# A two-block sequence model on one core: modulation columns of the first block summed on TensorE, the delta rule's inverse loaded by another queue

## The chip, the cores and the metric

The kernel runs on one NeuronCore of a Trainium2 chip, as one launch. The metric is device time in microseconds (us); lower is better. The core's engines work at the same time, each through its own list of instructions in a fixed order, and wait for one another through semaphores. TensorE is PE in the profile (PEld is its weight load), VectorE is DVE, ScalarE is ACT, GpSimd is POOL, and SyncE is SP. SP here only starts transfers; POOL starts transfers too, on a queue of its own.

## The reference, cut to what matters

Two blocks follow one another. The change lies in the first, which works on 1024 latent tokens and 256 context tokens of width 1024:

```
silu_c = silu(c)
sh1, sc1, g1, sh2, sc2, g2 = split(silu_c @ w_mod + b_mod, 6)      # 6 vectors of 1024
h  = rmsnorm(x, norm1_g) * (1 + sc1) + sh1
zl = h @ w_in ;  zc = hc @ w_in                                     # one projection for all mixers
y  = concat([hyena(zl_hy), gla(zl_gla, zc_gla), gdn(zl_gdn, zc_gdn)]) @ w_out
x  = x + g1 * y
x  = x + g2 * square(relu(modulate(x, norm2_g, sh2, sc2) @ w_mlp1)) @ w_mlp2

# gdn: gated delta rule, 4 heads, forward and backward, in chunks
a   = -(k*beta) @ k.T * exp(strict lower decay)
sol = solve(eye - a, [k*beta*exp(gcum), v*beta])                    # triangular solve
w, u = sol                                                          # then a scan over chunks
```

Hyena is a long convolution done with discrete Fourier tables, GLA is a gated linear attention, gdn is the gated delta rule. All numbers are float32; matrix products that need it are split into a high and a low part.

## The kernel before, in words

**Modulation.** Of the six vectors, four (g1, sc2, sh2, g2) are made by `mods1` with `mod_block`, one column block of 1024 of `w_mod` each. A column block comes in eight row blocks `mr` (128 x 1024, 512 KB), and with the `"pool"` setting ACT scales a block by its entry of silu(c) (L268), POOL adds it to a running sum `ma` (L391; the first of eight is written by ACT as `ma` itself), and at the end PE sums `ma` over partitions with eight products of a 128x128 piece of `ma` as weight and a column of ones (the trace's `px<-consts,ma`; each float32 product is two instructions). `mr` lies in two slots of the tag `wr`, `ma` in a slot of `wh`; both tags hold the weights of the projection before that and of the output product after.

**The delta rule.** `gdn_pre` first builds the strict matrices and stores them in HBM (`gdnU`, `gdnE`). Then, in the stage called E below, it goes over four heads h and two directions d, eight chains in all. Per head it loads keys and values (`st`, 96 x 1280, from SP), transposes them on PE into rows `rk` and `rv` (one buffer each). Per direction POOL makes `nk = rk * nbg` and `W = rv * beta` (L1240, L1241), and `gdn_E` loads `U` (L1144, from SP) and builds the inverse E by doubling the block size, 16 to 32 to 64 to 128: short products on PE (`D,U`, `E,Z`, `Ec,Z`), each followed by a copy on ACT or DVE, which the next products need. Then products with W and nk follow (`W,E`, `E,nk`), whose results POOL stores (`gdn_W` L1249, `gdn_GT` L1256). The end of `gdn_GT` is the end of a chain.

**What lies around it.** Hyena's Fourier products (`fh,TF`, `fl,TF`, `gh,TI`, `gl,TI`, with splits on DVE at L287) have their own input and no part in the delta rule; so have the modulation and, later, GLA's products (`eq`, `ek`, `v`, `at`, `kr`). The scan of the delta rule (two passes, W added at L1327, rows at L1351) needs all of E. Its result `orowsd` gets a head norm (ACT squares `hnj`, POOL L966), is transposed on PE, goes to HBM (`yT`, L979) and back as the input of the output product WO (`pm<-wo,cl` and `ch`).

**What sets the order.** The code is run at build time through a scheduler that puts each engine's instructions in one list, by priority and by when buffers come free. Every list is then executed in order. So an edit in one place shifts work of other parts in all lists: which Hyena, modulation or GLA products stand between two links of an E chain is decided there.

Of the kernel before, what the change touches and what calls it, by code (L numbers as in the profile page):

```python
# [19 lines left out]
D = 1024  # L20
# [3 lines left out]
KT = 8  # L24
# [142 lines left out]
class Builder:  # L167
# [204 lines left out]
    def mod_block(self, tl, w, b, cvs, outs, eng="dve"):  # L372


        nc, nv = self.nc, len(cvs)
        acc = [tl(f"ma{v}", 1, (128, D)) for v in range(nv)]
        for k in range(KT):
            raw = tl("mr", 2, (128, D))
            nc.sync.dma_start(out=raw, in_=w[k * 128 : (k + 1) * 128, :])
            for v in range(nv):  # L380
                cv = cvs[v][:, k : k + 1]
                if v == 0 and eng == "dve":
                    if k == 0:
                        self.ts(acc[0], raw, cv, ALU.mult)
                    else:
                        self.stt(acc[0], raw, cv, acc[0], ALU.mult, ALU.add)
                elif k == 0:
                    self.act(acc[v], raw, AF.Copy, scale=cv)
                else:
                    self.act(raw, raw, AF.Copy, scale=cv)  # L390
                    nc.gpsimd.tensor_add(out=acc[v], in0=acc[v], in1=raw)  # L391
            yield
        p = self.ps()
        for v in range(nv):
            for j in range(8):
                self.mm(p[:, v * 8 + j : v * 8 + j + 1], acc[v][:, j * 128 : (j + 1) * 128], self.ones[:, 0:1])
        for v in range(nv):
            nc.vector.tensor_add(out=outs[v], in0=p[:, v * 8 : v * 8 + 8], in1=b)
        yield
# [740 lines left out]
    def gdn_E(self, h, d, tl, ps, Ud, Ed, E, D1, Ec):  # L1140

        nc, V = self.nc, self.nc.vector
        U = tl("U", 2, (128, 10, 128))
        nc.sync.dma_start(out=U, in_=Ud[h, d].rearrange("c j i -> j c i"))  # L1144
        blk = lambda b: slice(b * 32, b * 32 + 32)
        v32 = lambda p: p[:, :320].rearrange("p (c t) -> p c t", t=32)
        flat = lambda t: t.rearrange("p c t -> p (c t)")
# [52 lines left out]

    def gdn_rows(self, src, dst):

        for c0 in range(0, 10, 5):
            p = self.ps()
            for i in range(5):
                self.tp(p[:, i * 96 : i * 96 + 96], src[:, (c0 + i) * 128 : (c0 + i + 1) * 128])
            self.act(dst[:, c0 : c0 + 5], p[:, :480].rearrange("p (c d) -> p c d", d=96), AF.Copy)

    def gdn_pre(self, dr, gt):
# [12 lines left out]
        with ExitStack() as es:  # L1222
# [6 lines left out]
            for h in range(4):  # L1229
                rows = []  # L1230
                for n in "kv":
                    t, r = tl("st", 2, (96, TT)), tl("r" + n, 1, (128, 10, 96))
                    nc.sync.dma_start(out=t, in_=dr[n][h * 96 : h * 96 + 96])
                    self.gdn_rows(t, r)
                    rows.append(r)
                for d in range(2):
                    E = Es[d]
                    f = lambda n: gt[n][:, d * 40 + h * 10 : d * 40 + h * 10 + 10].unsqueeze(2).broadcast_to([128, 10, 96])
                    nk, W = tl("nk", 1, (128, 10, 96)), tl("W", 2, (128, 10, 96))
                    nc.gpsimd.tensor_mul(out=nk, in0=rows[0], in1=f("nbg"))  # L1240
                    nc.gpsimd.tensor_mul(out=W, in0=rows[1], in1=f("beta"))  # L1241
                    self.gdn_E(h, d, tl, self.ps, Ud, Ed, E, D1[d], Ec[d])
                    G = tl("G", 1, (96, 10, 128))
                    for c0 in range(0, 10, 5):
                        p = self.ps()
                        for i in range(5):
                            self.mm(p[:, i * 96 : i * 96 + 96], E[:, c0 + i], W[:, c0 + i])
                        self.act(W[:, c0 : c0 + 5], p[:, :480].rearrange("p (c d) -> p c d", d=96), AF.Copy)
                    nc.gpsimd.dma_start(out=dr["W"][h, d], in_=W)  # L1249
                    for c0 in range(0, 10, 4):  # L1250
                        n = min(4, 10 - c0)
                        p = self.ps()
                        for i in range(n):
                            self.mm(p[:96, i * 128 : i * 128 + 128], nk[:, c0 + i], E[:, c0 + i])
                        self.act(G[:, c0 : c0 + n], p[:96, : n * 128].rearrange("p (c t) -> p c t", t=128), AF.Copy)
                    nc.gpsimd.dma_start(out=dr["GT"][h, d], in_=G)  # L1256
# [310 lines left out]
    def mods1(self, tl):  # L1567
# [2 lines left out]
        m = {}  # L1570
        for j, nm in ((2, "g1"), (4, "sc2"), (3, "sh2"), (5, "g2")):
            t = self.const(nm, [128, 8])
            for _ in self.mod_block(tl, A["w_mod"][0][:, j * D : j * D + D], self.c["b_mod"][:, j * 8 : j * 8 + 8], [c], [t], "pool"):
                pass
            m[nm] = self.col_row(nm + "row", t) if nm[0] == "g" else t
        m["gs2"] = self.gs_cols("gs2", m["sc2"], self.c["norm2_g"])
# [134 lines left out]
    def block1(self, x3, ey):  # L1711
# [16 lines left out]
        with ExitStack() as e1:  # L1728
# [60 lines left out]
            with ExitStack() as es:  # L1789
# [3 lines left out]
                ep.enter_context(self.psums(px=4))  # L1793
                with ExitStack() as eh:
                    hl = self.tiler(self.pool(eh, "hym"))
                    ml = lambda tag, bufs, shape: self.wp.tile(list(shape), F32, name=self.nm(tag), tag={"mr": "wr", "ma0": "wh"}[tag], bufs=2)
                    eh.enter_context(self.smalls())
                    self.hy_mix(F, dr["hy"], yT, hl)
                    pmix, self.pools = self.pools, pmod
# [692 lines left out]
```

## Time and profile before

| what | value |
|---|---|
| median of 3 runs | 3723.88 us (3720.07 to 3733.52) |
| profiled execution | 3723.89 us |
| span in its trace | 3722.1 us |
| mean granted TensorE clock | 0.914 |
| PE busy | 3350.3 us, 90% of the span |
| DVE, ACT, POOL busy | 63%, 42%, 36% |

The profiled execution is at the median, and its span is shorter than its time by 1.8 us. In the views a granted clock of 1 is 2.4 GHz and 0.5 is 1.2 GHz; a value between them is a mean over a stretch with both. The chain that ended last is given by the page for the whole span and only reaches back to about 1005 us; the stages of the first block before that are read from windows. In this execution the last product of the first block's projections ends at 626 us.

### The profile page before, as it was taken

How to read it: one execution, taken by the hardware profiler on the slowest of the kernel's cores; microseconds unless marked ns; L12 is line 12 of the kernel's file. 1: busy time of each engine (PE TensorE's matmuls, PEld its weight loads, DVE VectorE, ACT ScalarE, POOL GpSimd, SP SyncE). 2: the span in 40 equal slices, each digit the busy share in tenths (PEclk: the TensorE clock that was granted, in tenths of full speed). 3: DMA queues.
4: the chain of work that ended last, by engine and by line, in shares of the span. 5: the costliest groups of instructions: out<-in, count | busy, mean ns of one | idle time of the engine just before them, and what ended most of it. 6: DMA issues, size and time to landing. Idle time of an engine off the chain costs nothing.

```text
span 3722.1 us, 53759 instructions
## 1 busy us (share of the span) xinstructions
PE 3350.3 (90%) x19966; PEld 2797.4 (75%) x19966; DVE 2339.3 (63%) x4512; ACT 1563.9 (42%) x3045; POOL 1350.8 (36%) x1182
## 2 busy tenths in 40 slices
PE   6899998667796999999999799998899999998897
PEld 5567877567785777777788678887788778876785
DVE  8696452667457466456544756665677756664776
ACT  4454345533324252222211434444466554444663
POOL 3233344553546433234422201112555511113554
PEclk9799998767655999999999899999999999998998
DMA  7544544744313553222221111113444421124443
GB/s 258 183 143 148 141 127 148 236 153 140 106 42 102 187 183 92 70 88 91 85 84 47 62 38 57 50 50 90 138 121 144 156 63 60 49 66 137 116 134 139
DMA packets 350098, 421.24 MB, mean 113 GB/s; under 512 B 58388, under 2 KB 273860, under 8 KB 349837
## 3 DMA queue, kind: packets, MB, share of 16 engines
q1 hardware_dynamic: 323372, 322.21, 29.2%
q0 software_dynamic: 26464, 95.58, 7.0%
q8 instruction: 159, 2.61, 0.3%
q14 instruction: 103, 0.84, 0.1%
HBM read 317.96 MB, written 99.76 MB: 112 GB/s over the span
## 4 chain that ended last, share of the span: by engine, by line
PE 47%; DVE 10%; issue 5%; DMA 4%; ACT 4%; POOL 3%; SPq 0%; POOLq 0%; ACTq 0%; DVEq 0%
PE pm L256 28%; PE px L256 13%; PE pa L256 2%; PE po L256 1%; PE px L265 1%; PE pa L265 1%; DMA mr<-in_w_ada 1%; DVE ma L271 1%; ACT e L268 1%; DVE amx L2376 1%; DVE e L287 1%; DVE x L287 1%; DMA wr<-qd 1%; POOL ma L391 0%; POOL cl L287 0%
## 5 line engine op out<-in xcount | busy, mean ns | idle before, releaser
L256 PE MATMUL pm<-x,wh 128*128 128x512 f32 (+3 forms) x4768 | 1427.6, 380 | 2.3 <-DVE x L287 2.3
L256 PEld LDWEIGHTS pm<-x,wh 128*128 128x128 f32 (+2 forms) x4768 | 865.4, 189 | 164.3 <-issue 5.9
L256 PE MATMUL pm<-x,wl 128*128 128x512 f32 (+3 forms) x2384 | 909.4, 382 | 30.0 <-ACT u L268 21.0
L256 PEld LDWEIGHTS pm<-x,wl 128*128 128x128 f32 (+2 forms) x2384 | 451.7, 190 | 117.6 <-ACT u L268 21.7
L256 PE MATMUL pm<-wo,ch 128*128 128x512 f32 x832 | 267.3, 402 | 0.0
L287 DVE TENSOR_TENSOR wl<-wr,wh 128x1024 fp32r<-128x1024 f32 (+1 forms) x110 | 143.3, 1303 | 164.1 <-ACT wh L268 163.8
L1654 DVE TENSOR_TENSOR oa<-px,oa 128x512 f32<-128x512 f32 x240 | 161.7, 688 | 130.0 <-PE px L256 129.9
L391 POOL TENSOR_TENSOR ma<-ma,mr 128x1024 f32<-128x1024 f32 x63 | 160.5, 2548 | 178.5 <-ACT mr L268 154.0
L256 PE MATMUL px<-w2h,ml 128*128 128x512 f32 x480 | 195.4, 407 | 25.0 <-DVE ml L287 25.0
L268 ACT ACTIVATE u<-pm 128x512 f32<-128x512 f32 (+2 forms) x204 | 108.5, 543 | 258.0 <-PE pm L256 229.7
L256 PE MATMUL px<-w2h,mh 128*128 128x512 f32 x480 | 192.6, 401 | 0.0
L256 PE MATMUL px<-w2l,mh 128*128 128x512 f32 x480 | 192.1, 400 | 0.0
L256 PEld LDWEIGHTS pm<-wo,ch 128*128 128x128 f32 x832 | 160.1, 193 | 32.1 <-issue 0.2
L275 POOL TENSOR_SCALAR mkw<-kr,gws 128x128 f32<-128x128 f32 x144 | 80.7, 565 | 284.0 <-PE px L256 235.4
L256 PE MATMUL pm<-wo,cl 128*128 128x512 f32 x416 | 169.7, 408 | 9.9 <-POOL cl L287 8.0
L2376 DVE TENSOR_REDUCE amx<-pa 128x1 f32<-128x640 f32 (+2 forms) x144 | 107.4, 746 | 73.6 <-PE pa L256 72.5
L268 ACT ACTIVATE wh<-wr 128x1024 fp32r<-128x1024 f32 (+2 forms) x138 | 143.3, 1038 | 18.4 <-PE pm L256 13.9
L268 ACT ACTIVATE e<-e 128x1280 f32<-128x1280 f32 (+3 forms) x126 | 134.1, 1068 | 39.9 <-DVE e L275 36.8
L268 ACT ACTIVATE w2h<-wr 128x1024 fp32r<-128x1024 f32 x32 | 33.9, 1058 | 269.1 <-PE px L256 232.7
L268 ACT ACTIVATE P<-pa,amx 128x640 f32<-128x640 f32 (+2 forms) x144 | 105.6, 734 | 95.2 <-DVE amx L275 84.9
L268 ACT ACTIVATE mr<-mr,silu_cc 128x1024 f32<-128x1024 f32 x63 | 72.3, 1148 | 149.7 <-DVE ma L271 113.6
L1552 POOL TENSOR_TENSOR xr<-or,xr 128x512 f32<-128x512 f32 x72 | 93.4, 1297 | 103.0 <-DVE or L1551 87.0
(899 smaller groups left out, 7392.6 us busy)
## 6 DMA issues: line engine op xcount, KB each, us to landing
wr<-in_w_in SPq DMA_DIRECT2D x102, 512.0 KB
wr<-in_w_mlp SPq DMA_DIRECT2D x64, 512.0 KB
mr<-in_w_ada SPq DMA_DIRECT2D x48, 512.0 KB
TF<-dft SPq DMA_DIRECT2D x54, 384.0 KB
mr<-in_w_mod SPq DMA_DIRECT2D x32, 512.0 KB
xp<-xr POOLq DMA_DIRECT2D x26, 512.0 KB, 4.0
xr<-xp SPq DMA_DIRECT2D x26, 512.0 KB
wr<-in_w_out SPq DMA_DIRECT2D x24, 512.0 KB
```

Source lines behind the costliest of these rows:

```text
L256: self.nc.tensor.matmul(out, a, b, start=start, stop=stop)
L265: self.nc.tensor.transpose(out, in_, self.ident[:p, :p])
L268: self.nc.scalar.activation(out, in_, f, **kw)
L271: self.nc.vector.scalar_tensor_tensor(out=out, in0=in0, scalar=scalar, in1=in1, op0=op0, op1=op1)
L275: (eng or self.nc.vector).tensor_scalar(out=out, in0=in0, scalar1=s1, scalar2=s2, op0=op0, **kw)
L287: (leng or self.nc.vector).tensor_sub(out=lo, in0=src, in1=hi.bitcast(F32))
L391: nc.gpsimd.tensor_add(out=acc[v], in0=acc[v], in1=raw)
L1552: nc.gpsimd.tensor_add(out=xr[:, fs], in0=r, in1=xr[:, fs])
L1654: V.tensor_add(out=oa[t][:, fs], in0=p, in1=oa[t][:, fs])
L2376: V.reduce_max(m_, s[:, w0:768], axis=AX.X)
```

## The change

There are four edits. With `"pe"`, `mod_block` sums on TensorE: each 128x128 piece of a row block `mr` is the weight of a product with the one matching column of silu(c), eight pieces for each of eight row blocks, 64 columns of PSUM in all, which DVE reduces over k and adds the bias to. ACT's scaling and POOL's sums are gone for these four vectors. The row blocks take turns in the two tags `wr` and `wh` of two slots each. `U` is loaded by POOL's queue. `rk` and `rv` have two buffers each and are loaded in halves, and for d = 1 POOL scales them in place, where before a separate `nk` and `W` were written.

```diff
 def mod_block(self, tl, w, b, cvs, outs, eng="dve"):
+        if eng == "pe":
+            p = self.ps()[:, :64]
+            for k in range(KT):
+                raw = tl(k, (128, D))
+                nc.sync.dma_start(out=raw, in_=w[k * 128 : (k + 1) * 128, :])
+                for j in range(8):
+                    self.mm(p[:, j * 8 + k : j * 8 + k + 1], raw[:, j * 128 : (j + 1) * 128], cvs[0][:, k : k + 1])
+                yield
+            nc.vector.reduce_sum(outs[0], p.rearrange("p (j k) -> p j k", k=KT), axis=AX.X)
+            nc.vector.tensor_add(out=outs[0], in0=outs[0], in1=b)
+            yield
+            return
...
 def gdn_E(self, h, d, tl, ps, Ud, Ed, E, D1, Ec):
-        nc.sync.dma_start(out=U, in_=Ud[h, d].rearrange("c j i -> j c i"))
+        nc.gpsimd.dma_start(out=U, in_=Ud[h, d].rearrange("c j i -> j c i"))
...
 def gdn_rows(self, src, dst):
-        for c0 in range(0, 10, 5):
+        for c0 in range(0, dst.shape[1], 5):
...
 def gdn_pre(self, dr, gt):
-                    t, r = tl("st", 2, (96, TT)), tl("r" + n, 1, (128, 10, 96))
-                    nc.sync.dma_start(out=t, in_=dr[n][h * 96 : h * 96 + 96])
-                    self.gdn_rows(t, r)
+                    r = tl("r" + n, 2, (128, 10, 96))
+                    for c0 in (0, 5):
+                        t = tl("st", 2, (96, 640))
+                        nc.sync.dma_start(out=t, in_=dr[n][h * 96 : h * 96 + 96, c0 * 128 : c0 * 128 + 640])
+                        self.gdn_rows(t, r[:, c0 : c0 + 5])
...
-                    nk, W = tl("nk", 1, (128, 10, 96)), tl("W", 2, (128, 10, 96))
+                    nk, W = rows if d else (tl(t, 1, (128, 10, 96)) for t in ("nk", "W"))
...
         for j, nm in ((2, "g1"), (4, "sc2"), (3, "sh2"), (5, "g2")):
             t = self.const(nm, [128, 8])
-            for _ in self.mod_block(tl, A["w_mod"][0][:, j * D : j * D + D], self.c["b_mod"][:, j * 8 : j * 8 + 8], [c], [t], "pool"):
+            for _ in self.mod_block(tl, A["w_mod"][0][:, j * D : j * D + D], self.c["b_mod"][:, j * 8 : j * 8 + 8], [c], [t], "pe"):
...
                     hl = self.tiler(self.pool(eh, "hym"))
-                    ml = lambda tag, bufs, shape: self.wp.tile(list(shape), F32, name=self.nm(tag), tag={"mr": "wr", "ma0": "wh"}[tag], bufs=2)
+                    ml = lambda k, shape: self.wp.tile(list(shape), F32, name=self.nm("mr"), tag=("wr", "wh")[k % 2], bufs=2)
```

What this does to the lists shows at three places. The first is PE at the end of the chain of head 1, direction 1. Before, the links of the chain (`px_46..`, products with E, Z, nk and W) stand between Hyena's products (TF, TI):

```order
L256 MATMUL px_4643<-E_781_3684,Z_4561 64x64 x5
L256 MATMUL px_4651<-W_4454,E_781_3684 128x96 x5
L256 MATMUL px_8288<-fh_8284,TF_8282 128x512
L256 MATMUL px_8310<-gh_8304,TI_8308 128x256
...
L256 MATMUL px_8288<-fl_8285,TF_8282 128x256
L256 MATMUL px_8288<-fh_8284,TF_8282 128x256
L256 MATMUL px_4658<-W_4454,E_781_3684 128x96 x5
L256 MATMUL px_4666<-E_781_3684,nk_4453 96x128 x4
```

In the changed kernel the same links have products of the modulation (`silu_cc,mr`) between them as well as Hyena's:

```order
L256 MATMUL px_9248<-silu_cc,mr_9279 128x1 x2
L256 MATMUL px_4647<-E_781_3684,Z_4565 64x64 x5
L256 MATMUL px_4655<-rv_4210,E_781_3684 128x96 x5
L256 MATMUL px_9248<-silu_cc,mr_9279 128x1
L256 MATMUL px_8450<-gh_8444,TI_8448 128x512
L256 MATMUL px_9248<-silu_cc,mr_9279 128x1 x2
L256 MATMUL px_9248<-silu_cc,mr_9289 128x1 x7
L256 MATMUL px_8450<-gl_8445,TI_8448 128x512
L256 MATMUL px_8450<-gh_8444,TI_8448 128x512
L256 MATMUL px_8450<-gh_8444,TI_8448 128x256
L256 MATMUL px_8450<-gl_8445,TI_8448 128x256
L256 MATMUL px_4662<-rv_4210,E_781_3684 128x96 x5
```

Hyena is further on at this place (its product 8450 against 8288), and all products of the modulation, 256 against 32, stand between the last projection and the end of the last chain; the rest of Hyena's, which before stood in the scan (107 of 300 rows), stand there too.

The second is POOL around the same chain. Before, the running sums `ma` stand between the multiplications of the delta rule and its stores:

```order
L391 TENSOR_TENSOR ma_1748_9150<-ma_1748_9150,mr_9178 128x1024
L1249 DMA gdn_W<-W_4224 128x960
L391 TENSOR_TENSOR ma_1760_9199<-ma_1760_9199,mr_9203 128x1024
L1240 TENSOR_TENSOR nk_4453<-rk_4190,gnbg_2320 128x960
L1256 DMA gdn_GT<-G_4420 96x1280
```

In the changed kernel no sum is left, and the loads of U (L1156) stand between:

```order
L1156 DMA U_4729<-gdnU 128x10x128
L1263 DMA gdn_W<-W_4230 128x960
L1270 DMA gdn_GT<-G_4426 96x1280
L420 DMA g1row<-crow_9243 8x128
L1156 DMA U_4957<-gdnU 128x10x128
L1263 DMA gdn_W<-rv_4210 128x960
L1270 DMA gdn_GT<-G_4654 96x1280
L1254 TENSOR_TENSOR nk_4725<-rk_4687,gnbg_2320 128x960
L1254 TENSOR_TENSOR rk_4687<-rk_4687,gnbg_2320 128x960
L1255 TENSOR_TENSOR W_4726<-rv_4706,gnbeta_2277 128x960
L1255 TENSOR_TENSOR rv_4706<-rv_4706,gnbeta_2277 128x960
```

A load of U for a later chain stands ahead of the stores of the chain that runs, and the four multiplications of a head (in place for d = 1) follow one another.

The third is PE between the end of the scan and WO. Before, the last transposes of `orowsd` are followed by GLA's products, 195 with eq and ek and 33 with v, S or kr among them, and the first product of WO comes after the last of them:

```order
L265 MATMUL px_8174<-consts,orowsd 128x128 x4
L256 MATMUL px_10561<-eq_10473,k_10026 128x128 x4
L256 MATMUL px_10596<-v_10035,at_1962_10334 128x96
...
L256 MATMUL pq_10658<-eq_10648,ek_10649 32x32
L256 MATMUL pq_10659<-eq_10648,ek_10649 32x32
L256 MATMUL pm_10276<-wo_1930_10212,cl_10269 128x512
```

In the changed kernel the scan's last products (S, W, qs) and the transposes stand directly ahead of WO:

```order
L256 MATMUL px_8051<-S_8029,qs_7692 128x96
L256 MATMUL px_8051<-W_8041,at_7691 128x96
L265 MATMUL px_8143<-consts,orowsd 128x128
...
L265 MATMUL px_8173<-consts,orowsd 128x128
L265 MATMUL px_8182<-consts,orowsd 128x128
L256 MATMUL pm_10448<-wo_1926_10384,cl_10441 128x512
```

GLA's products that stood here are in the scan now (496 rows with eq and ek there against 293), except the last twelve steps of the scan, which have none between them.

## Rows read from the trace of the kernel before

**Rows 1.** The page: busy us per engine, share of the span, instructions.

```profile
PE 3350.3 (90%) x19966; PEld 2797.4 (75%) x19966; DVE 2339.3 (63%) x4512; ACT 1563.9 (42%) x3045; POOL 1350.8 (36%) x1182
```

**Rows 2.** Windows: busy us (instructions) per engine, then clock, DMA share, GB/s.

```profile
627.00:858.00 231.00, 161.15 (x2185) 146.48 (x2186) 149.47 (x212) 103.72 (x182) 124.46 (x65) 0.67 0.60 188
858.00:988.00 130.00, 93.12 (x592) 85.01 (x590) 92.11 (x179) 40.01 (x79) 55.29 (x29) 0.77 0.50 141
988.00:1132.00 144.00, 137.15 (x1111) 119.11 (x1109) 73.90 (x192) 41.91 (x83) 67.24 (x48) 0.60 0.17 45
1132.00:1202.00 70.00, 42.42 (x457) 34.45 (x456) 53.56 (x70) 32.83 (x114) 51.14 (x33) 0.56 0.30 96
```

**Rows 3.** Line L1256, the store that ends each chain: ns, first and last start.

```profile
L1256 POOL DMA_DIRECT2D gdn_GT<-G x8: 523/547/710, 564.3 to 858.2; - x8
```

**Rows 4.** Waits, 627 to 858: us in total, times, longest.

```profile
PEld px L256 <- issue: 44.4, 15, 11.0
...
PE px L256 <- DVE D L1162: 22.6, 3, 10.9
```

**Rows 5.** Tile ma, window 627 to 858: columns as in rows 2.

```profile
627.00:858.00 231.00, 9.41 (x64) 9.55 (x64) 0.00 (x0) 3.43 (x3) 62.29 (x25) 0.67 0.60 188
```

**Rows 6.** Timelines of PE from 750 and from 803: start, duration.

```profile
750.60 1.84 PE L256 MATMUL px<-consts,ma 128*128 128x1 f32 x16
...
803.07 3.57 PE L256 MATMUL px<-consts,ma 128*128 128x1 f32 x16
```

**Rows 7.** Windows of 20 and 40 us: columns as in rows 2.

```profile
1060.00:1080.00 20.00, 20.00 (x223) 17.84 (x222) 10.58 (x28) 6.07 (x13) 8.25 (x7) 0.50 0.17 41
720.00:740.00 20.00, 16.14 (x186) 14.03 (x186) 15.95 (x27) 13.84 (x24) 9.48 (x4) 0.83 0.74 233
1220.00:1260.00 40.00, 40.00 (x221) 32.52 (x218) 16.84 (x26) 6.26 (x10) 17.02 (x17) 1.00 0.60 207
```

**Rows 8.** Tiles TF, then TI, window 858 to 988: PE, PEld, clock, DMA.

```profile
858.00:988.00 130.00, 11.50 (x45) 9.13 (x45) 0.77 0.50 141
...
858.00:988.00 130.00, 13.22 (x59) 10.59 (x57) 0.77 0.50 141
```

**Rows 9.** One DVE group by form, 627 to 858, then 858 to 988: busy, mean ns.

```profile
L287 DVE TENSOR_TENSOR gl<-t,gh 128x512 fp32r<-128x512 f32 x13 | 15.7, 1211 | 5.5 <-ACT gh L268 5.4
...
L287 DVE TENSOR_TENSOR gl<-t,gh 128x512 fp32r<-128x512 f32 x5 | 3.4, 682 | 0.8 <-ACT gh L268 0.8
```

**Rows 10.** Lines L1144 (U's load, SP) and L1109 (U's store, POOL): issue, ns min/median/max.

```profile
L1144 SPq DMA_DIRECT2D U<-gdnU x8: 370/376/5219, 481.3 to 777.6; - x8
...
L1109 POOL DMA_DIRECT2D gdnU<-U x8: 954/982/1418, 391.2 to 450.7; - x8
```

**Rows 11.** Groups by form, 1132 to 1202, PE, then ACT: busy, mean ns, idle before.

```profile
L265 PE MATMUL px<-consts,orowsd 128*128 128x128 f32 x24 | 6.2, 429 | 0.0
...
L256 PE MATMUL px<-v,kr 128*64 128x96 f32 x40 | 4.1, 365 | 11.8 <-ACT kr L268 7.8 <-DVE hnr L307 4.0
...
L268 ACT ACTIVATE hnj<-orowsd 128x96 f32<-128x96 f32 x29 | 7.8, 269 | 0.0
L268 ACT ACTIVATION_READ_ACCUMULATOR hnj<-orowsd 128x1 f32 x29 | 5.5, 189 | 0.0
```

**Rows 12.** Timeline of POOL, 1130 to 1203: start, duration, idle before.

```profile
1160.50 7.67 POOL L966 TENSOR_TENSOR orowsd<-orowsd,hnr 128x384 f32<-128x384 f32 x8 [0.82 <-DVE hnr L307]
...
1195.95 1.56 POOL L898 TENSOR_TENSOR eq<-eq,q 128x512 f32<-128x512 f32 x1 [10.39 <-ACT eq L268]
...
1200.88 1.54 POOL L287 TENSOR_TENSOR cl<-wr,ch 128x640 fp32r<-128x640 f32 x1
```

**Rows 13.** The chain that ended last, around 1290: start, duration, what.

```profile
1288.01 6.38 DMA yT<-hng
1294.53 2.90 DMA wr<-yT
```

**Rows 14.** Line L1327 in the scan, 934 to 953: ns, first and last start.

```profile
L1327 DVE TENSOR_TENSOR W<-px,W x8: 347/358/358, 936.2 to 951.0; 128x192 f32<-128x192 f32 x8
```

## The prediction

> **What bounds the kernel now.** I read the page first. PE is busy nine tenths of the span and no other engine comes near it [rows 1], so the whole kernel is a list of PE's work with a few holes, and an edit can only be worth what it adds to that list or what it takes from the holes. The page's slices put the holes between a sixth and a third of the span, so next I cut that part into windows by stage [rows 2]: from the end of the projections to the end of the last E chain (627 to 858), the scan's part with Hyena beside it (858 to 988), the scan's part with GLA beside it (988 to 1132), and from the scan's end to the first product of WO (1132 to 1202). PE is idle there for 69.9, 36.9, 6.9 and 27.6 us, 141 of 575. All four edits act inside these 575 us. What comes after them has the same work as before, but for 8 GLA products fewer, so I take its time as unchanged.
>
> In the E stage the eight chains end between 564 and 858 us [rows 3], six of them behind the projections, so one takes 31 to 48 us. PE waits there for short copies that the next link of the chain needs: 22.6 us for D on DVE in three waits, and 44.4 us of weight loads wait for something that the profile does not show [rows 4]. PE does not wait for the modulation. So the chain of links, with whatever stands between them in PE's list, sets this stage.
>
> **The change part by part.** All sums are made in the time of the profiled execution, 3723.89 us, which is the median of the runs within 0.01 us.
>
> *Modulation on PE.* The order has 256 products where there were 32, all of them in the E stage. A product is two instructions, so 448 instructions are new. Before, 64 of this shape (a 128x128 weight, one column) took 9.41 us of that window, 0.147 us each [rows 5]. That mean lies between two levels in the timeline: 16 of them took 1.84 us at one place, 0.115 each, and 3.57 us at another, 0.223 each [rows 6], the ratio of the two clock levels. So the new work costs 448 x 0.147 = 65.9 us, with bounds of 51.5 and 99.9 us. I take the mean of the stage, because the new products are spread over all of it as the old ones were. What goes in exchange is POOL's sums and ACT's scaling, 62.3 us of POOL in this window [rows 5]; PE had no wait for these, so I count them at nothing directly.
>
> *What POOL's silence gives.* While POOL adds, some DVE operations of the same shape are longer: Hyena's low part `gl` took 1211 ns in the E stage and 682 ns in the scan [rows 9]. That is 13 x 0.53 = 7 us on DVE for this group. It shortens waits and not PE's work; I put it into the idle time below.
>
> *Hyena moves forward.* In the order none of Hyena's products is left in the scan. In the trace those were 11.50 + 13.22 = 24.7 us of PE [rows 8]. The E stage gets them and the scan loses them.
>
> *The E stage, summed.* PE's work becomes 161.2 + 65.9 + 24.7 = 251.8 us, more than the 231 us that the stage has. The idle time of 69.9 us cannot stay, because at most links there are now products to do. Some must stay, because the list is in order: a product that stands behind a link cannot go ahead of it, and six chains have about ten links each. I take 25 us, about 4 us for each chain; bounds are 0 and the old 69.9. The stage is then 276.8 us, **+45.8 us**.
>
> *U's load by POOL's queue, rows in two buffers and in place.* SP's issue of U's load took 0.37 us, once 5.2 us; POOL's issue of the store of the same tensor took about 1 us [rows 10]. Eight of these are 8 us on an engine that loses 62 us of sums, so the cost is nothing while POOL has slack. In POOL's list they stand ahead of the stores of the chain that is running, which then wait too if U's buffer is not free. The doubled rows let a head's transposes and multiplications be done while the head before it is still in its chains; this takes a start-up wait from each head, and I count that in the 25 us too. With the cover gone, a load of U that is late holds the first link of a chain: that is a rival below.
>
> *The scan.* Of 274 us PE was busy for 93.1 + 137.2 = 230.3. It loses Hyena's 24.7. It gains the GLA products that stood between the scan's end and WO: the 42.4 us of that window [rows 2] less the 6.2 us of the transposes, which stay [rows 11], 36.2 us. That makes 241.8 us. Of the idle 43.8 us I keep 33: GLA's products now fill more steps, but the last twelve steps have nothing beside them. Such bare steps were in the trace too; eight additions of W between 936.2 and 951.0 [rows 14] give about 2.1 us for a step, most of it PE's own. The scan is then 274.8 us, **+0.8 us**, with bounds of -17 (15 us idle) and +19. The upper one is the clock: if the part from 858 on falls from 0.77 to the 0.60 of the next window when Hyena leaves, its other 68.4 us of work grow by 28%, 19 us.
>
> *The scan's end to WO.* What held WO for 70 us was GLA's work in all lists: PE's products, and POOL's `eq` ahead of the split `cl` that WO's first product reads [rows 12]. PE alone waited 11.8 us for GLA's `kr` [rows 11]. With that work gone ahead, the head norm's own chain is left: the squares on ACT, 7.8 + 5.5 = 13.3 us if none is done in the scan [rows 11], POOL's scaling 7.67 us [rows 12], four transposes at 0.43 us, the store to `yT` with its landing 6.38 and the load back 2.90 [rows 13], the split 1.54 us: 33.5 us. Without the squares it is 20 us, but the small steps of the norm's root, not in this sum, come on top. I take 33 us, **-37 us**, with bounds of -50 and -20.
>
> The sum is 45.8 + 0.8 - 37 = +9.6 us: **3734 us**.
>
> **The rivals.**
>
> *The clock rises (faster).* The E stage ran at a granted clock of 0.67 on average. Where Hyena's wide products were dense it was 0.83, with PE busy for 16.1 of 20 us [rows 7]. If filling the holes brings the whole stage to that, its other work of 161.2 + 24.7 = 185.9 us shrinks by 0.67/0.83 to 150 us, the modulation costs its lower bound of 51.5, and with 25 us idle the stage is 226.5 us, 4.5 us less than before. With the scan and the tail as above that is -41 us: 3683 us. Against it: PE was busy for all of 1060 to 1080 at a clock of 0.50, with GLA's narrow products, and for all of 1220 to 1260 at 1.00 with WO's wide ones [rows 7]. So being busy did not by itself raise the clock here, and the new products are the narrowest of all. It decides from a stage mean of about 0.75 on. The Trainium skill, "TensorE: Matmul & The Clock Gate", section "What's actually happening", says that the default state is throttled and that activity releases it, to 2.4 GHz; by that rule this rival would be the forecast. The trace does not agree at 1060 to 1080, where PE has no hole and stays at the lower level.
>
> *The holes take everything.* The chance to be near 0 idle in the E stage: 251.8 us, +20.8, with the other terms -15.4 us: 3708 us. For it speaks that the new products wait for nothing but a load made long before; against it, the order of the list.
>
> *Half clock throughout (slower).* If the new products come in groups between links where the clock is low, as at 803 us, they cost 99.9 instead of 65.9 us: +34, 3768 us. It decides when more than half of them take over 0.2 us.
>
> *U late on POOL (slower).* If each load of U after the projections waits as long as SP's longest, 5.2 us, with the stores and the next head's multiplications behind it, six chains lose 31 us: 3765 us. Against it: POOL's queue has 62 us less to do, and the loads stand a chain ahead.
>
> *The tail keeps another holder.* If WO comes only 20 us earlier, for its low bound above, the total is 3751 us.
>
> **How the numbers follow.** About 0.5% (18.6 us) is what a measurement of this kernel can tell from no change; so faster is under 3705 and slower over 3742. The forecast, from 3715 to 3753 by the idle time in the E stage and in the scan, has a chance of 0.40; 0.30 of it lies within the bound and 0.10 above. The clock's rise has 0.24, all faster. The holes that take everything have 0.10, 0.06 of it faster. Half clock has 0.16, U late and the tail 0.05 each, all slower. That is 0.30 faster, 0.34 the same, 0.36 slower. For the range I go to the clock's rise below and to half clock above, each with some room for the scan's bounds: 3675 to 3785. The likeliest case's own range is 3715 to 3753.
>
> **What the profile would show.** *Modulation:* 512 instructions of one column with silu(c) in the E stage, their mean between 0.12 and 0.22 us, and PE's busy time there over 240 us; if the mean is at 0.115 and the stage's clock above 0.75, the clock's rise was right. *E stage:* its end (the last `gdn_GT`) about 46 us later, near 904, and PE idle in it under 30 us. *POOL:* no `ma`; if its waits ahead of the load of U are longer than a few us, and PE waits for that load, U is late. *DVE:* `gl` near 0.7 us in the E stage. *Scan:* from the last `gdn_GT` to its last W about 275 us. *Tail:* 33 us from there to WO's first product, with no GLA product in it, and the head norm and the transfer of `yT` as what is waited for. The forecast is wrong if the E stage's end moves by less than 20 us or more than 70, or if the tail stays over 50 us.

## The result and the profile after

The changed kernel takes 3787.27 us (median of 4 runs, 3775.92 to 3793.42) against 3728.70 us of the kernel before on the same chip: a ratio of 1.0149, 95% interval 1.0125 to 1.0173. It is slower by 1.5%, 58.6 us. The profiled execution after took 3781.57 us with a span of 3779.8, 57.7 us more than the span before, so the two traces show nearly all of the difference.

I cut both traces at the same events: the end of the projections, the last `gdn_GT` store, the last row that DVE adds to `orowsd`, the first product of WO, the end.

| stage | before, us | after, us | difference | forecast |
|---|---|---|---|---|
| up to the end of the projections | 625.8 | 627.6 | +1.8 | 0 |
| E stage | 232.4 | 288.7 | +56.3 | +45.8 |
| scan | 274.0 | 295.5 | +21.5 | +0.8 |
| scan's end to WO | 70.3 | 43.0 | -27.3 | -37 |
| from WO on | 2519.6 | 2525.0 | +5.4 | 0 |

From WO on I had forecast no change. In the traces of the experiments below this part (the span less the start of WO's first product) lasts between 2521 and 2530 us whatever the edit, so these 5.4 us can't be told from no change.

The page's first line after the change. PE's busy time grew by 89 us, POOL's fell by 71:

```profile
PE 3439.7 (91%) x20414; PEld 2885.2 (76%) x20414; DVE 2304.4 (61%) x4516; ACT 1533.2 (41%) x3013; POOL 1279.4 (34%) x1162
```

Windows by stage, with the columns of [rows 2]:

```profile
627.00:916.00 289.00, 264.17 (x2833) 249.01 (x2831) 166.23 (x290) 89.59 (x182) 74.51 (x48) 0.66 0.54 176
916.00:1212.00 296.00, 249.70 (x2040) 219.04 (x2040) 161.59 (x365) 91.61 (x201) 140.47 (x96) 0.66 0.24 64
1212.00:1255.00 43.00, 6.53 (x25) 4.47 (x26) 17.06 (x20) 16.03 (x68) 25.08 (x19) 0.53 0.50 161
```

In the E stage PE is idle for 24.8 us, where it was idle for 69.9 [rows 2]: the holes were filled, and the work that filled them was larger than the holes. The first row below gives that work; the second, the store that ends each chain, answers to [rows 3] with its last start 58 us later:

```profile
L256 PE MATMUL px<-silu_cc,mr 128*128 128x1 f32 x512 | 87.8, 299 | 0.0
...
L1270 POOL DMA_DIRECT2D gdn_GT<-G x8: 521/531/533, 564.3 to 916.3; - x8
```

512 instructions in 87.8 us are 0.171 each (the 299 ns are the overlapping durations of single ones). The weights' loads take as long, 89.3 us of PEld beside 87.8 of PE. The granted clock of the stage hardly moved, 0.66 for 0.67. The new products are found at both levels again, as in [rows 6]; in the timeline of PE after, 0.213 us each in the first row and 0.116 in the second:

```profile
821.60 2.98 PE L256 MATMUL px<-silu_cc,mr 128*128 128x1 f32 x14
...
844.31 1.62 PE L256 MATMUL px<-silu_cc,mr 128*128 128x1 f32 x14
```

Windows of 30 us show where the scan gained idle time: in its first 60 us, after the change and before it, with the columns of [rows 2].

```profile
916.00:946.00 30.00, 12.57 (x70) 11.74 (x70) 8.23 (x20) 7.00 (x12) 14.30 (x10) 0.60 0.81 221
946.00:976.00 30.00, 15.31 (x195) 13.08 (x197) 24.05 (x42) 9.18 (x17) 22.80 (x13) 0.65 0.22 64
```

```profile
858.00:888.00 30.00, 24.53 (x138) 21.64 (x136) 24.12 (x42) 12.74 (x26) 9.27 (x5) 0.77 0.70 205
888.00:918.00 30.00, 21.91 (x141) 19.86 (x142) 27.49 (x46) 10.26 (x20) 13.34 (x7) 0.89 0.30 77
```

PE is idle for 32.1 us there, before for 13.6. The timeline after says what it waits for. SP's list has GLA's tables and first loads ahead of the scan's keys; all are issued only after the last store of the E stage, and PE stands until the keys have landed:

```profile
918.90 0.33 SPq L210 DMA_DIRECT2D consts<-in_consts  x1
919.28 0.77 SPq L827 DMA_DIRECT2D v<-gla_v  x1
920.15 1.10 SPq L831 DMA_DIRECT2D lk<-gla_log  x1
921.30 0.43 SPq L1293 DMA_DIRECT2D k<-gdn_k  x1
...
932.12 1.83 PE L265 MATMUL px<-consts,k 96*128 96x96 f32 x10 [17.14 <-DMA k<-gdn_k]
```

SP's own waits from 890 to 945 after the change say what held it: GLA's tables (`consts`), ahead of the keys in its list, wait for the landing of a store of Hyena's result (`yT<-EO`), which the moved Hyena now makes at the end of the E stage.

```profile
SPq L210 <- DMA yT<-EO: 21.4, 1, 21.4
```

Before, the keys were issued behind the last store too, at 858.89. But PE had products of Hyena to do until they had landed, and took the keys with no wait:

```profile
858.89 0.42 SPq L1279 DMA_DIRECT2D k<-gdn_k  x1
...
862.07 0.80 PE L256 MATMUL px<-fh,TF 128*128 128x512 f32 x1 [3.58 <-ACT fh L268]
...
868.73 0.99 PE L265 MATMUL px<-consts,k 96*128 96x96 f32 x10
```

Behind the scan all of GLA's work is gone from PE's list, as the order said, and WO still waits 18.2 us for `cl`. The timeline of POOL after shows what stands ahead of `cl`: besides the norm's scaling (L978) and the stores to `yT`, the multiplications of WO's weights by g1 (L1577), which wait for their loads.

```profile
1225.75 2.34 POOL L1577 TENSOR_TENSOR wr<-wr,g 128x1024 f32<-128x1024 f32 x1 [4.42 <-DMA wr<-in_w_out]
1228.04 7.30 POOL L978 TENSOR_TENSOR orowsd<-orowsd,hnr 128x384 f32<-128x384 f32 x8
...
1235.31 4.64 POOL L1577 TENSOR_TENSOR wr<-wr,g 128x1024 f32<-128x1024 f32 x2
...
1239.90 1.37 POOL L991 DMA_DIRECT2D yT<-hng  x2
...
1253.21 1.55 POOL L287 TENSOR_TENSOR cl<-wr,ch 128x640 fp32r<-128x640 f32 x1
```

### The profile page after: what moved, and what is told of

Same layout as the page of the kernel before. It is cut to its first block, busy times and chain, and to the rows that moved or that the text cites. A ratio compares the mean times of both kernels' runs of the same rounds, so it can differ in the third digit from the quotient of the medians.

```text
span 3779.8 us, 54585 instructions
## 1 busy us (share of the span) xinstructions
PE 3439.7 (91%) x20414; PEld 2885.2 (76%) x20414; DVE 2304.4 (61%) x4516; ACT 1533.2 (41%) x3013; POOL 1279.4 (34%) x1162
## 4 chain that ended last, share of the span: by engine, by line
PE 63%; DVE 14%; issue 6%; DMA 6%; ACT 5%; POOL 4%; SPq 0%; POOLq 0%; ACTq 0%; DVEq 0%
PE pm L256 35%; PE px L256 22%; PE pa L256 2%; PE px L265 2%; PE po L256 1%; DVE ma L271 1%; DMA mr<-in_w_ada 1%; PE pa L265 1%; DVE ac L271 1%; ACT e L268 1%; DVE x L287 1%; DMA wr<-in_w_out 1%; POOL ma L403 1%; DMA wr<-in_w_in 1%; DVE e L287 1%
## 5 line engine op out<-in xcount | busy, mean ns | idle before, releaser
L256 PE MATMUL pm<-x,wh 128*128 128x512 f32 (+3 forms) x4768 | 1429.1, 381 | 1.8 <-DVE x L287 1.8
L256 PEld LDWEIGHTS pm<-x,wh 128*128 128x128 f32 (+2 forms) x4768 | 866.5, 189 | 162.6 <-issue 5.5
L256 PE MATMUL pm<-x,wl 128*128 128x512 f32 (+3 forms) x2384 | 910.2, 382 | 27.8 <-ACT u L268 21.0
L256 PEld LDWEIGHTS pm<-x,wl 128*128 128x128 f32 (+2 forms) x2384 | 452.1, 190 | 115.5 <-ACT u L268 22.1
L256 PE MATMUL pm<-wo,ch 128*128 128x512 f32 x832 | 268.9, 403 | 0.0
L256 PE MATMUL px<-w2h,ml 128*128 128x512 f32 x480 | 194.6, 405 | 25.8 <-DVE ml L287 17.5
L256 PE MATMUL pm<-wo,cl 128*128 128x512 f32 x416 | 170.4, 410 | 25.4 <-POOL cl L287 24.6
L256 PE MATMUL px<-w2l,mh 128*128 128x512 f32 x480 | 191.4, 399 | 0.0
L256 PE MATMUL px<-w2h,mh 128*128 128x512 f32 x480 | 191.4, 399 | 0.0
L256 PEld LDWEIGHTS pm<-wo,ch 128*128 128x128 f32 x832 | 160.9, 194 | 32.6 <-issue 0.2
L403 POOL TENSOR_TENSOR ma<-ma,mr 128x1024 f32<-128x1024 f32 x35 | 90.0, 2571 | 126.9 <-ACT mr L268 111.7
L256 PEld LDWEIGHTS px<-w2h,ml 128*128 128x128 f32 x480 | 93.0, 194 | 49.0 <-DVE ml L287 19.2
```

Source lines behind the costliest of these rows:

```text
L256: self.nc.tensor.matmul(out, a, b, start=start, stop=stop)
```

## The experiments

Three theories stood at first: the products on TensorE are the loss; U's load on POOL is, since POOL waited 57 us ahead of it in the E stage (the first row of that stage's list of POOL's waits, `POOL U L1156 <- PE px L256: 57.0, 3, 27.9`); the moved order is. The first four kernels take the change apart.

**The modulation back on POOL, the other edits kept.**

```diff
-            for _ in self.mod_block(tl, A["w_mod"][0][:, j * D : j * D + D], self.c["b_mod"][:, j * 8 : j * 8 + 8], [c], [t], "pe"):
+            for _ in self.mod_block(tl, A["w_mod"][0][:, j * D : j * D + D], self.c["b_mod"][:, j * 8 : j * 8 + 8], [c], [t], "pool"):
-                    ml = lambda k, shape: self.wp.tile(list(shape), F32, name=self.nm("mr"), tag=("wr", "wh")[k % 2], bufs=2)
+                    ml = lambda tag, bufs, shape: self.wp.tile(list(shape), F32, name=self.nm(tag), tag={"mr": "wr", "ma0": "wh"}[tag], bufs=2)
```

> The changed kernel with the modulation of before (scaled on ACT, summed on POOL); U by POOL's queue and the doubled rows stay. First theory (the modulation on TensorE is the whole loss, 87.8 us of narrow products in a stage that has no holes for them): 3700 to 3735 us, the time of before or a little less, E stage 225 to 235 us long. Second theory (U's load blocks POOL's queue, which waited 57 us ahead of it): over 3750 us, with the wait ahead of U's load still there and PE waiting in the E stage.

Measured: 3736.32 us, 1.0019 (1.0001 to 1.0037). E stage 231.8 us, scan 277.3, tail 63.5. The loss is nearly gone with the modulation. At 1 us over the first theory's range, a rest of some 7 us stays with the other edits. Hyena's products stand in the scan again, 21.7 us of them in its first 60, where PE is idle for 14.7 us:

```profile
861.30:921.30 60.00, 45.35 (x287) 41.13 (x287) 52.21 (x88) 21.54 (x44) 24.03 (x12) 0.85 0.46 134
```

**The modulation on TensorE alone.** The kernel before with the new branch of `mod_block` and these lines:

```diff
-            for _ in self.mod_block(tl, A["w_mod"][0][:, j * D : j * D + D], self.c["b_mod"][:, j * 8 : j * 8 + 8], [c], [t], "pool"):
+            for _ in self.mod_block(tl, A["w_mod"][0][:, j * D : j * D + D], self.c["b_mod"][:, j * 8 : j * 8 + 8], [c], [t], "pe"):
-                    ml = lambda tag, bufs, shape: self.wp.tile(list(shape), F32, name=self.nm(tag), tag={"mr": "wr", "ma0": "wh"}[tag], bufs=2)
+                    ml = lambda k, shape: self.wp.tile(list(shape), F32, name=self.nm("mr"), tag=("wr", "wh")[k % 2], bufs=2)
```

> The kernel before with the modulation on TensorE and its four weight slots alone. First theory: as slow as the changed kernel or a little slower, 3780 to 3800 us, since rows are not doubled. Second theory (U's load on POOL costs): clearly faster than the changed kernel, 3730 to 3760 us.

Measured: 3767.61 us, 1.0099 (1.0072 to 1.0126), below the range of the first theory and above that of the second. E stage 278.7 us, scan 302.8 at a clock of 0.60, as this window of the scan shows:

```profile
898.60:1201.40 302.80, 263.74 (x2038) 231.96 (x2035) 158.67 (x365) 92.68 (x203) 141.17 (x97) 0.60 0.22 58
```

So two thirds of the loss, 38 us, are the modulation's by itself, and the rest needs another of the edits. These 38 and the 7 us of the run before do not add up to 58.6: the edits act on one another.

**U loaded by SP again.**

```diff
-        nc.gpsimd.dma_start(out=U, in_=Ud[h, d].rearrange("c j i -> j c i"))
+        nc.sync.dma_start(out=U, in_=Ud[h, d].rearrange("c j i -> j c i"))
```

> The changed kernel with U loaded by SP again. First theory: within 10 us of the changed kernel, 3777 to 3797 us. Second theory: 20 to 50 us faster than the changed kernel.

Measured: 3782.78 us, 1.0141 (1.0113 to 1.0168), the changed kernel within the interval. The second theory falls: POOL's long wait ahead of U holds nothing that is needed sooner.

**Half of the products.**

```diff
-                for j in range(8):
+                for j in range(8 if k % 2 == 0 else 0):
...
```

The columns of PSUM and the sum over k shrink with it.

> The changed kernel with only the even four of eight row blocks multiplied (128 products for 256; all blocks are still loaded; the sums lack half their terms). The order keeps Hyena wholly in the E stage and GLA in the scan. First theory, by the duration of a product: 256 instructions of 0.171 us less, 44 us, so about 3743 us, with the E stage near 246 us and the scan and the tail unchanged. Third theory (the loss is the moved order, not the products): over 3770 us. If the holes would have taken the products: less than 15 us gained.

Measured: 3733.35 us, 1.0022 (0.9997 to 1.0047), 54 us less than the changed kernel. The profiled execution is the slowest of its twelve (3719 to 3765), so its stages show less of the gain than the medians do; in it the E stage is 254.7 us, 34.0 less, the tail 43.3 as in the changed kernel, and the scan 303.2, 7.7 more, at a clock of 0.62 for 0.66. With the order kept, the time of the products comes back; the third theory, by which the time stays over 3770, falls.

This kernel also parts the late keys of the scan from the missing Hyena. Its scan has none of Hyena's products either, but SP issued the keys 10 us before the last store of the E stage (887.1), and PE hardly waited for them. Still it is idle for 25.1 of the scan's first 60 us; the rows are the keys' issue, PE's wait for them, and that window:

```profile
877.29 0.42 SPq L1293 DMA_DIRECT2D k<-gdn_k  x1
...
PE px L265 <- DMA k<-gdn_k: 0.7, 1, 0.7
...
887.10:947.10 60.00, 34.86 (x239) 32.06 (x237) 35.10 (x68) 15.59 (x31) 36.36 (x21) 0.77 0.57 159
```

The products then became the point to work on. Each loads a weight of 128x128 for a single column. **Turned round**, the column is the weight and the row block moves:

```diff
-                for j in range(8):
-                    self.mm(p[:, j * 8 + k : j * 8 + k + 1], raw[:, j * 128 : (j + 1) * 128], cvs[0][:, k : k + 1])
+                for q in range(4):
+                    self.mm(p[q * 32 : q * 32 + 32, :256], cvs[0][:, k : k + 1].broadcast_to([128, 32]),
+                            raw[:, q * 256 : (q + 1) * 256], k == 0, k == KT - 1)
...
+            t = self.small([128, 256], "mrow", 1)
+            nc.vector.tensor_copy(out=t, in_=p[:, :256])
+            for r in range(2):
+                self.tp(p[:, 256 + r * 128 : 384 + r * 128], t[:, r * 128 : r * 128 + 128])
```

Of the two transposes every 32nd column is taken, and the bias is added. In the changed kernel:

> The changed kernel with the operands of the modulation turned round: the column of silu(c), repeated to 32 columns, is the weight, a quarter of a row block (256 columns) is what moves, and four such products write four groups of 32 partitions; 256 instructions for 512, and two transposes for each vector bring the row to a column. First theory (the narrow products, at 0.171 us each by their 128x128 weights, are the loss): if four neighbouring products overlap as the 32x32 products of the chains do, about 0.05 us each, 13 us in all, the kernel comes to 3700 to 3735 us; if they follow one another at 0.213 us or more, 55 us or more in all, 3750 to 3780 us. Third theory (the moved order is the loss): over 3770 us unless the order moves back; in this order 53 of 300 rows of Hyena stand in the scan and 144 rows of GLA behind it.

Measured: 3725.28 us, 0.9988 (0.9969 to 1.0008), 62 us less than the changed kernel: within the range for products that overlap. By itself this run does not part the products from the order, which moved back in part (its tail is 64.3 us long again); half of the products did. In the kernel before, as its only edit:

> The kernel before with the turned modulation on TensorE alone; U on SP and the rows single. If the doubled rows and U's queue cost 10 to 20 us beside a modulation on TensorE, as the changed kernel's 3787 against 3768 for the modulation alone say, this is 10 to 20 us faster than the changed kernel with the turned products; if those 20 us were a matter of how full the stage is, it is the same within 8 us.

Measured: 3704.09 us, 0.9928 (0.9908 to 0.9948), faster than both kernels and 21 us faster than the kernel with all edits. So the other edits cost some 20 us beside the turned products too, in a stage that is less full. The group of the turned products in this kernel's E stage, and 24 of them in its timeline:

```profile
L256 PE MATMUL px<-mr,silu_cc 128*32 128x256 f32 x256 | 22.8, 450 | 2.6 <-DMA mr<-in_w_mod 2.3 <-DVE sh L388 0.3
...
620.23 1.50 PE L256 MATMUL px<-mr,silu_cc 128*32 128x256 f32 x24
```

They take 22.8 us in all for 87.8, 0.089 each, and in this row 0.063, though each alone lasts 378 ns or more in the trace: the products overlap. The E stage, in the columns of [rows 2], has the higher clock; it starts 6 us earlier than in the kernel before and ends 28 us earlier:

```profile
620.00:830.00 210.00, 167.56 (x2426) 139.91 (x2414) 135.19 (x224) 77.27 (x159) 58.36 (x37) 0.74 0.65 215
```

The rest asked which of the other edits costs 20 us. **Narrow products and U by POOL, rows as before:** the kernel with the modulation on TensorE alone, and

```diff
-        nc.sync.dma_start(out=U, in_=Ud[h, d].rearrange("c j i -> j c i"))
+        nc.gpsimd.dma_start(out=U, in_=Ud[h, d].rearrange("c j i -> j c i"))
```

> The kernel before with the modulation on TensorE (narrow, as in the change) and U by POOL's queue; the rows stay single and are written to buffers of their own. The order on TensorE is that of the modulation alone. If U's queue is free, 3768 us as the modulation alone, within 8 us, and the doubled rows in place are what costs the rest up to 3787. If U's queue costs, 3780 us or more.

Measured: 3766.05 us, 1.0092 (1.0068 to 1.0116): U's queue costs nothing here, and the rows cost the rest. Their parts one by one, on the kernel with the turned products alone (3704 us). **Rows in two buffers, loaded in halves, not in place:**

```diff
-                    t, r = tl("st", 2, (96, TT)), tl("r" + n, 1, (128, 10, 96))
+                    r = tl("r" + n, 2, (128, 10, 96))
+                    for c0 in (0, 5):
+                        t = tl("st", 2, (96, 640))
...
```

> The kernel before with the turned modulation, and rk and rv in two buffers, loaded in halves; nk and W are still written to buffers of their own, and U is loaded by SP. The turned modulation alone took 3704 us, with doubled rows, in place and U's queue 3725. If the doubled rows bring the loss, by the other order that the scheduler makes of them (237 rows of Hyena in the E stage for 201): 3715 to 3735 us. If not, 3698 to 3710.

Measured: 3720.18 us, 0.9979 (0.9963 to 0.9994), as expected if this part brings the loss. **In place alone:**

```diff
-                    nk, W = tl("nk", 1, (128, 10, 96)), tl("W", 2, (128, 10, 96))
+                    nk, W = rows if d else (tl(t, 1, (128, 10, 96)) for t in ("nk", "W"))
```

> The kernel before with the turned modulation, and for d = 1 the rows scaled in place; rk and rv keep one buffer, so the transposes of the next head must wait until the products of d = 1 have read them. If the scaling in place brings the loss of 21 us (later starts of a head): 3715 us or more, with the chains of a head's start later by some us each. If not, 3698 to 3710.

Measured: 3700.76 us, 0.9927 (0.9913 to 0.9941): no cost. **U by POOL's queue alone:**

```diff
-        nc.sync.dma_start(out=U, in_=Ud[h, d].rearrange("c j i -> j c i"))
+        nc.gpsimd.dma_start(out=U, in_=Ud[h, d].rearrange("c j i -> j c i"))
```

> The kernel before with the turned modulation, and U by POOL's queue. With the narrow products U's queue made no difference (3766 for 3768, and 3787 for 3783), so 3698 to 3712 us. If U's queue costs where the E stage is shorter, since POOL then waits for U's buffer ahead of its stores: 3715 us or more.

Measured: 3715.47 us, 0.9958 (0.9938 to 0.9979), on the side of a cost, but unclear: its twelve executions lie between 3694.43 us at a granted clock of 0.924 and 3728.17 at 0.912, its interval overlaps that of the kernel without the edit (0.9908 to 0.9948), and the rows of PE's order have the same counts by kind in every stage. **Two weight slots for four**, on the kernel with the rows in place:

```diff
-                    ml = lambda k, shape: self.wp.tile(list(shape), F32, name=self.nm("mr"), tag=("wr", "wh")[k % 2], bufs=2)
+                    ml = lambda k, shape: self.wp.tile(list(shape), F32, name=self.nm("mr"), tag="wr", bufs=2)
```

> The turned modulation with rows in place, as in the run before (3701 us), but with the row blocks of w_mod in two weight slots instead of four. If four slots matter, the products come later in the E stage, wait for their loads, and the kernel takes 3706 us or more. If the loads are far enough ahead anyway, 3694 to 3706.

Measured: 3702.00 us, 0.9922 (0.9901 to 0.9944): the two further slots make no difference. **Loads in halves, one buffer each**, on the kernel with both:

```diff
-                    r = tl("r" + n, 2, (128, 10, 96))
+                    r = tl("r" + n, 1, (128, 10, 96))
```

> The turned modulation, with keys and values loaded in halves but rk and rv in one buffer each. The order on TensorE is row for row that of the doubled rows, which took 3720 us. If the halves (twice as many loads, and the other order made of them) are what costs there, 3712 to 3728 us; if it was the second buffer itself, 3698 to 3708.

Measured: 3713.38 us, 0.9968 (0.9947 to 0.9990), inside the range for the halves. It lies 9 us over the kernel without them and 7 under the one with both buffers; its interval touches the first one's and overlaps the second's. The halves carry a part of the cost; whether the second buffers carry any is not resolved.

## Why the prediction held only at the edge of its range

The measured 3787 us lies 2 us above the upper end of the range, 3785, in this comparison's runs; by the ratio and the median of before that the prediction started from (1.0149 x 3723.88 = 3779.4) it is inside. The forecast of the likeliest, +9.6 us (within what can be told), was wrong by 49 us. That the range reached so far is in part luck: its upper end was made for half clock in the E stage with some room for the scan, and of the 48 us that the traces lie over the forecast the E stage gave only 10.5; the scan gave 20.7, the tail 9.7, the stages ahead and behind 7. Step by step:

*Modulation, mis-sized.* "So the new work costs 448 x 0.147 = 65.9 us" was the right mechanism at too low a price. They came to 87.8 - 9.4 = 78.4 us, 12.5 more, since the mean of the stage was 0.171 us and not 0.147: more of them stood at the lower clock level. By an estimate from the two prices at the levels, 0.116 and 0.213 here and 0.115 and 0.223 in [rows 6], over half of them did, for three in ten before. So the rival of half clock came true in part, for 12.5 of its 34 us. Halving the products took 34.0 us off the stage, 0.133 us for each of 256 instructions, though they themselves took 43.6 less (44.2 for 87.8): PE's idle time in the stage rose from 24.8 to 41.8, so the holes that come back take up a part of what leaves.

*Holes in the E stage, right.* I took 25 us of idle time, it was 24.8. PE's work was forecast at 251.8 us and was 264.2; the difference is the products' price.

*POOL's silence, right for the group that I read.* The low part `gl` on DVE fell from 1211 ns [rows 9] to 720 in the E stage, as in this group of the profile after (count, busy us, mean ns):

```profile
L287 DVE TENSOR_TENSOR gl<-t,gh 128x512 fp32r<-128x512 f32 x18 | 12.9, 720 | 5.4 <-ACT gh L268 5.2
...
L287 DVE TENSOR_TENSOR fl<-Y,fh 128x256 fp32r<-128x256 f32 x4 | 9.5, 2410 | 0.1
```

The mean hides what happens: the median of `gl` is 692 ns in both traces, and a few long ones raise the mean, up to 2497 ns before and 1256 after. The second row shows that it is not the sums alone. The narrow `fl` took 2668 ns each before and still 2410 with no sum on POOL, but 419 in the kernel with the modulation back on POOL. All four stand beside a multiplication for Hyena on POOL in the timeline after; two of them:

```profile
657.18 4.90 POOL L705 TENSOR_TENSOR hx<-hx,hd 128x2048 f32<-128x2048 f32 x1 [3.69 <-issue]
...
657.87 4.83 DVE L287 TENSOR_TENSOR fl<-Y,fh 128x256 fp32r<-128x256 f32 x2
```

So POOL's other work does the same as the sums. That POOL causes it is read from such pairs of rows, and what decides between a long and a short one was not tested.

*The clock's rise, wrong as a rival.* The stage was granted 0.66 with PE busy for 264 of 289 us. By the Trainium skill's rule ("TensorE: Matmul & The Clock Gate", section "What's actually happening"), by which activity releases the throttle, it should have risen; the trace of this stage does not agree, with 0.67 before and 0.66 after. In the kernel with the turned products alone the stage had 0.74. Whether the kind of products did this, or the other order beside them, was not tested apart.

*U late on POOL, did not come.* POOL waited for U's buffer longer than feared, 57.0 us in three waits for the 31 of the rival, but loading U from SP again gave 4 us, inside the noise. What stood behind the waiting load was not needed sooner. Beside the turned products a cost of U's queue is not settled (3715 for 3704, unclear).

*The scan, the step that failed.* "The scan is then 274.8 us, +0.8 us" was wrong by 20.7 us: its idle time was about 46 us for 33, and PE's work 249.7 us for 241.8. I had taken Hyena's 24.7 us out of the scan as time and had not named what they cover, and I had kept the idle time for the last bare steps. These cost 2.37 us each (in PE's timeline their first products start at 1198.99, 1201.36 and 1203.73 us), near the 2.1 forecast, but only 0.45 us of each was idle. The idle time stood at the other end. All of Hyena's 24.7 us had lain in the scan's first 60 us, and when they left, PE's idle time there rose by 18.5 us, from 13.6 to 32.1; with the modulation back on POOL, and Hyena back in the scan, it is 14.7.

The late keys are a part of this and not all of it. PE waited 17.1 us for them, because Hyena's last store held up SP's list. In the kernel with half of the products, where the keys came early, the idle time was still 25.1 us; in the kernel with the modulation on TensorE alone, where they were issued at 884.20, 14 us before the last store, it was 28.7. By these two the late keys are worth 3 to 7 of the 18.5 us. The rest, as the waits read, is that the scan's first steps wait for one another with too little else in PE's list there: PE's longest waits in the second kernel's window are 11.4 us for a copy of S on DVE and 7.5 for `kw` on POOL. That the work came out 7.9 us longer is of a size that the clock moves: almost the same list took 249.7 us at 0.66 here and 263.7 at 0.60 there.

*Tail, right in kind, 10 us short.* It fell by 27.3 us to 43.0, within the bounds of -50 and -20. Of my chain, I left out that POOL multiplies WO's weights by g1 ahead of the norm's scaling and of `yT`'s store: 2.34 + 4.64 us, and the waits for their loads.

*Rows in two buffers and in halves, counted at nothing, cost 15 to 21 us beside a modulation on TensorE.* With the narrow products 3783 for 3768 and 3787 for 3766, with the turned ones 3720 for 3704; beside the modulation on POOL all the other edits together cost 7. In place and four slots cost and give nothing. How the rows cost is open. The profiled executions of the two kernels with halves, with other parts of Hyena in the E stage, differ from the one without by only 3 to 6 us in span, the medians by 9 to 16 (one of these two executions is the fastest of its twelve). The runs' granted clock is lower in the median, 0.914 and 0.916 for 0.920. I could not tell the order's part from the clock's.

## What to carry to other kernels

A hole in the busiest engine is filled only up to its size: add up the new work with the price at the clock of that very stage, against the idle time of that stage. Where a planner moves work out of a stage, ask what that work was covering there, waits between the stage's own steps as well as loads: here 18.5 of the 24.7 us that left came back as idle time. A product of a vector with a matrix was cheap on TensorE here with the vector as the weight: four groups of 32 columns made the modulation almost four times cheaper (22.8 for 87.8 us) and the kernel 0.7% faster than before, where the form with the matrix as the weight made it 1% slower as the only edit.

## What the runs showed of the hardware

Products of 256 columns with weights of 128x32, to four groups of 32 output partitions, overlap: 24 of them in 1.50 us, though each lasts 0.38.

The kernel with the turned products and U by POOL's queue ran, in twelve executions, between 3694.43 us at a mean granted clock of 0.924 and 3728.17 us at 0.912, 34 us apart, on one chip. The kernel with the turned products alone stayed between 3696 and 3713, in six executions on another chip. A single profiled execution stood 0.6% from the median of its runs in that kernel and 0.8% in the one with half of the products, which is as much as the smaller edits here were worth.

An operation on DVE can last several times as long beside one on POOL: four low parts `fl` of 128x256 took 2410 ns each in the changed kernel, all beside a multiplication on POOL, and 419 in the kernel with the modulation back on POOL.
